# Ten adaLN sections as row sums on VectorE, in a two-layer backbone kernel on one Trainium2 core

## The chip, the core and the metric

The kernel runs on one core of a Trainium2 chip. The core has engines that work side by side, each through its own instructions in program order: TensorE (PE, matrix products), VectorE (DVE), ScalarE (ACT), GpSimd (POOL), and SyncE (SP), whose queue issues the transfers (DMA) from device memory. They meet by semaphores. The metric is the device time of one launch in microseconds. Of the kernel before there are three timed runs and one profiled execution, in which every instruction's start and length was recorded.

## What is computed

Two layers over 256 context and 256 latent tokens of width 1024. Each layer first turns two condition vectors, `c` for the latent tokens and `c_ctx` for the context, into six sections of 1024 numbers: shift, scale and gate of the mixing (0, 1, 2) and of the feed-forward part (3, 4, 5).

```python
silu_c, silu_cc = silu(c), silu(c_ctx)
for layer in range(2):
    mod_l = silu_c  @ ada_w[layer] + ada_b[layer]     # [1024] @ [1024, 6144]
    mod_c = silu_cc @ ada_w[layer] + ada_b[layer]
    sh1, sc1, g1, sh2, sc2, g2 = split(mod, 6)        # for latent and context tokens each
    h = rms_norm(x, norm1_g) * (1 + sc1) + sh1
    x = x + g1 * (concat(A(h), B(h), C(h)) @ w_out)   # three groups of attention heads
    h = rms_norm(x, norm2_g) * (1 + sc2) + sh2
    x = x + g2 * (swiglu(h) if layer == 0 else moe(h))  # dense, 2816 wide; top 2 of 8 experts
return rms_norm(x_latent, final_g)
```

`ada_w` of one layer is 1024 x 6144 floats, 24 MB; the whole of it serves two vectors.

## The kernel before

The tokens are kept feature-major (`xT`, eight k-tiles of 128 features by 512 tokens). All large products are made from high and low parts: `Weights` loads raw columns into the ring `raw` (two places), ACT copies the high part (`whi`, L219), DVE subtracts it from the raw for the low part (`wlo`, L385), and `mm3` multiplies in three passes (L645 to L647). So DVE has to make a low part of 128x512 for every k-tile of weights before PE can do the third pass of it. High and low parts have two places each.

The work is written as pieces. `add(engine, us, f, after, rank, take, give)` puts a piece on a list; `Plan`, a list scheduler with estimated durations, fixes the order: whenever an engine is free, it takes the first in rank of the pieces whose needs are met and whose buffers (`take`) are free. A smaller rank goes first. The order found is then the order of each engine's instructions and doesn't change at run time. Layer 0's mixing has ranks from 0, the pieces for its gaps 5000 (`FILL`) and on, the dense feed-forward part 6000 and on (its chunks 100 apart, each half 1000), layer 1's mixing 10000 and on. After layer 1's mixing come the experts, in an order written by hand.

The modulation is made by `ada(l, b0, nb, rings, rank, after)` for `nb` blocks of 128 columns of `ada_w[l]`. It loads eight k-tiles into tiles `idle`; PE multiplies each with `sil` (the two vectors, silu applied, as the first two of 32 columns), k-tile 4i + g into column group g of PSUM (`adap`, L442, eight matmuls in each of two pieces); ACT copies the result (`adar`); PE transposes it, one transpose a block (`adat`, L452); DVE adds the four groups (L456) and the bias (L457) into `mods[l]`. There are 42 calls:

- eight at the start, for sections 0 and 1 of layer 0, with tiles of the ring `long`;
- thirteen of two blocks each in layer 0's mixing, for its blocks 16 to 41, with rank 5000 + block and a tile of the ring `raw`;
- thirteen in the feed-forward part, twelve of three blocks and one of two, for layer 0's blocks 42 to 47 and layer 1's blocks 0 to 31: two calls follow each chunk of hidden activations and one each half of the down projection's columns, with the rank of that chunk plus 12, behind the chunk's own products and weights, and two tiles of the ring `mixC`;
- eight of two blocks in layer 1's mixing, for its blocks 32 to 47.

The dense part goes in two halves g of 1408 hidden columns; each has three chunks (gate and up products, `fsg` = silu(gate) times up at L1658, its high and low parts `fhh`, `fhl`) and then the down projection in two halves of columns, whose sums go into `xT` with the gate of `mods`.

## Time and profile before

| | |
|---|---|
| three timed runs | median 1942.58 us (1941.44 to 1943.14) |
| profiled execution, span | 1941.8 us |
| PE busy | 1904.0 us, 98% |
| DVE busy | 1427.7 us, 74% |
| ACT busy | 1170.6 us, 60% |
| DMA, mean rate | 243 GB/s |

The span runs from the first to the last recorded instruction. "Busy" is the time in which an engine executed something other than waits, branches and DMA issues; matmuls are pipelined, so that one can start before the one ahead of it ends, and the distance from start to start tells more than a single length. The page of the profile gives averages; tables by stretch of time, timelines and lists of waits are read from the trace of the same execution.

### The profile page before, as it was taken

The numbers are of one execution on the slowest core, as the hardware profiler recorded it, in microseconds if no ns is written. First come the engines' busy times: TensorE is split into PE (matmuls) and PEld (weight loads), VectorE is DVE, ScalarE is ACT, GpSimd is POOL, SyncE is SP. The second block draws the span as 40 slices with busy tenths as digits, with TensorE's granted clock in tenths as the row PEclk, the third lists the DMA queues.
The fourth block names the chain that finished last, engine by engine and source line by source line (L and its number), as shares of the span: only waits on it lengthen the run. The fifth ranks groups of instructions, "written<-read, shape, count | busy, mean of one in ns | idle before, by whom it ended". The sixth has DMA issues, their size and how long they took to land.

```text
span 1941.8 us, 27786 instructions
## 1 busy us (share of the span) xinstructions
PE 1904.0 (98%) x10317; PEld 1562.8 (80%) x10317; DVE 1427.7 (74%) x2330; ACT 1170.6 (60%) x1938; POOL 38.9 (2%) x44
## 2 busy tenths in 40 slices
PE   7999999999999999999999999999999999999998
PEld 4988678877787799887788888888888888888886
DVE  5564987433333345768889998999989999899997
ACT  4443684332222334448777777777777777777776
POOL 1001100000000000020000000000000000000000
PEclk9999999999999999999999999999999999999999
DMA  9313532435434423257799999999999999999991
GB/s 301 102 55 100 182 104 84 155 131 190 141 121 140 148 73 97 83 161 238 281 353 369 363 371 332 356 364 370 373 333 354 372 365 376 327 358 373 373 367 36
DMA packets 268911, 474.41 MB, mean 244 GB/s; under 512 B 14440, under 2 KB 75584, under 8 KB 268640
## 3 DMA queue, kind: packets, MB, share of 16 engines
q1 hardware_dynamic: 268384, 472.37, 69.6%
q8 instruction: 83, 1.36, 0.3%
q0 software_dynamic: 384, 0.19, 0.1%
q14 instruction: 60, 0.49, 0.1%
HBM read 471.47 MB, written 1.05 MB: 243 GB/s over the span
## 4 chain that ended last, share of the span: by engine, by line
PE 94%; DMA 2%; DVE 2%; ACT 1%; issue 0%; SPq 0%; DVEq 0%; ACTq 0%
PE gu L2110 32%; PE py L2135 16%; PE acc L645 9%; PE acc L647 8%; PE acc L646 8%; PE adap L442 2%; PE acc L855 2%; DMA idle<-in_ada_w 2%; PE acc L857 2%; PE acc L856 2%; PE pT L1241 1%; PE mtp L2124 1%; PE oBp L1329 1%; PE gth L2020 1%; PE sct L2159 1%; PE poC L1074 1%
## 5 line engine op out<-in xcount | busy, mean ns | idle before, releaser
L1845 DVE TENSOR_TENSOR mlo<-early,mhi 128x512 fp32r<-128x512 f32 (+1 forms) x350 | 340.0, 1019 | 24.6 <-issue 18.3
L219 ACT ACTIVATE mhi<-early 128x512 fp32r<-128x512 f32 (+1 forms) x352 | 291.3, 885 | 49.0 <-PE py L2135 25.1
L385 DVE TENSOR_TENSOR wlo<-raw,whi 128x512 fp32r<-128x512 f32 (+4 forms) x292 | 150.5, 564 | 157.8 <-ACT whi L219 157.0
L2110 PE MATMUL gu<-mlo,xh 128*128 128x512 f32 x896 | 247.9, 395 | 0.0
L219 ACT ACTIVATE whi<-raw 128x512 fp32r<-128x512 f32 (+4 forms) x292 | 134.9, 525 | 181.5 <-PE acc L646 146.5
L2110 PE MATMUL gu<-mhi,xh 128*128 128x512 f32 x896 | 244.0, 391 | 0.0
L2110 PE MATMUL gu<-mhi,xl 128*128 128x512 f32 x896 | 243.1, 390 | 0.0
L2135 PE MATMUL py<-mhi,hid 128*128 128x512 f32 x896 | 235.3, 390 | 0.0
L645 PE MATMUL acc<-hhi,whi 128*128 128x512 f32 (+1 forms) x576 | 217.6, 378 | 2.8 <-DVE rC L885 1.9
L646 PE MATMUL acc<-hlo,whi 128*128 128x512 f32 (+1 forms) x576 | 210.7, 366 | 2.2 <-DVE hlo L579 2.2
L647 PE MATMUL acc<-hhi,wlo 128*128 128x512 f32 (+1 forms) x576 | 210.6, 366 | 0.5 <-DVE wlo L385 0.5
L1845 DVE TENSOR_TENSOR mlo<-more,mhi 128x1024 fp32r<-128x1024 f32 (+1 forms) x174 | 198.5, 1184 | 11.9 <-issue 10.6
L2110 PEld LDWEIGHTS gu<-mhi,xl 128*128 128x128 f32 x896 | 168.2, 188 | 35.9
L2135 PEld LDWEIGHTS py<-mhi,hid 128*128 128x128 f32 x896 | 167.7, 188 | 35.6
L2110 PEld LDWEIGHTS gu<-mhi,xh 128*128 128x128 f32 x896 | 167.4, 188 | 34.4
L2110 PEld LDWEIGHTS gu<-mlo,xh 128*128 128x128 f32 x896 | 164.4, 188 | 31.5
L219 ACT ACTIVATE mhi<-more 128x1024 fp32r<-128x1024 f32 (+1 forms) x174 | 169.0, 1022 | 28.2 <-PE py L2135 28.2
L1845 DVE TENSOR_TENSOR mlo<-mraw,mhi 128x1024 fp32r<-128x1024 f32 (+1 forms) x116 | 132.5, 1186 | 15.6 <-ACT mhi L219 8.5
L1845 DVE TENSOR_TENSOR mlo<-spare,mhi 128x1024 fp32r<-128x1024 f32 x108 | 127.3, 1220 | 15.3 <-PE py L2135 8.0
L645 PEld LDWEIGHTS acc<-hhi,whi 128*128 128x128 f32 x576 | 108.8, 189 | 35.3 <-issue 11.2
L646 PEld LDWEIGHTS acc<-hlo,whi 128*128 128x128 f32 x576 | 108.9, 189 | 18.9 <-DVE hlo L579 3.1
L647 PEld LDWEIGHTS acc<-hhi,wlo 128*128 128x128 f32 x576 | 108.7, 189 | 18.7 <-DVE wlo L385 0.9
(371 smaller groups left out, 3035.2 us busy)
## 6 DMA issues: line engine op xcount, KB each, us to landing
early<-in_moe_w_up SPq DMA_DIRECT2D x56, 1024.0 KB, 6.0
more<-in_moe_w_up SPq DMA_DIRECT2D x54, 1024.0 KB, 6.2
early<-in_moe_w_gate SPq DMA_DIRECT2D x52, 1024.0 KB, 6.5
spare<-in_moe_w_down SPq DMA_DIRECT2D x48, 1024.0 KB, 6.0
early<-in_moe_w_down SPq DMA_DIRECT2D x112, 256.0 KB, 6.1
mraw<-in_moe_w_gate SPq DMA_DIRECT2D x27, 1024.0 KB, 6.2
mraw<-in_moe_w_down SPq DMA_DIRECT2D x27, 1024.0 KB, 5.7
more<-in_moe_w_gate SPq DMA_DIRECT2D x24, 1024.0 KB, 6.3
```

The lines of the kernel that those rows point to most:

```text
L219: act(o, i, AF.Copy)
L385: tt(l_, v, h, op=OP.subtract)
L442: mm(w["pm"][32 * g:32 * g + 32, :n], sil[:, 4 * i + g, :], w["raw"][4 * i + g], start=i == 0, stop=i == 1, tile_position=(0, 32 * g))
L645: mm(o, lh, rh, start=start, stop=False)
L646: mm(o, lh, rl, start=False, stop=False)
L647: mm(o, ll, rh, start=False, stop=stop)
L855: mm(p, t["hi"][:, kk, s], w.w[0][:, k, :], start=kk == 0, stop=False)
L856: mm(p, t["hi"][:, kk, s], w.w[1][:, k, :], start=False, stop=False)
L857: mm(p, t["lo"][:, kk, s], w.w[0][:, k, :], start=False, stop=kk == KD - 1)
L1845: tt(l, w, h, op=OP.subtract)
L2110: mm(out, a[kk // 2][:, kk % 2, o:o + 128], b[:, k, :], start=i + kk == 0, stop=i == 2 and kk == KD - 1)
L2135: mm(out, a[:, k, :], b[:, k, :], start=i + c + k == 0, stop=i == 2 and c == NCH - 1 and k == 3)
```

## The change

Sections 0 and 1 of layer 0 are made as before, by the first eight calls of `ada`. All other calls are gone: the thirteen in layer 0's mixing, the thirteen in the feed-forward part and the eight in layer 1's mixing. In their place stands `ada_rows(l, sec, rank, after)`, called in layer 0's mixing for sections 2 to 5 of layer 0 and then 0 to 5 of layer 1, ten calls, with ranks 5000 to 5009; their loads follow one another and begin behind a load of the projection's weights.

For each half of 512 columns of a section, `ada_rows` loads the eight k-tiles two at a time (512 KB, ring `adw`, two places). On DVE each k-tile is multiplied with its column of `sil`, once for each of the two vectors, and added to a running sum `adacc` (one place for a pair of sums). Then each sum is transposed in blocks of 32 x 32 and reduced over 32 columns into `adsum`. When both halves are done, one matmul with a new constant `four` (ones where row and column agree modulo 32) adds the four groups of 32 partitions, and DVE adds the bias in four instructions of 32 x 16. A section has 4 tensor_scalar, 28 scalar_tensor_tensor, 4 transposes, 4 reductions and 4 additions on DVE and one matmul on PE. An unused tile of the ring `work` is dropped, and a scratch size of the DMAs is set to 4096 bytes, which frees memory for the new rings.

```diff
@@ constants @@
+    c["four"] = p[:, None] % 32 == p[None, :] % 32
@@ kernel @@
-    plan = Plan(big=2, sm=4, hi=2, lo=2, raw=2, sp=2, work=10, long=24, mixC=2, b16=2, units=5, oC=2)
+    plan = Plan(big=2, sm=4, hi=2, lo=2, raw=2, sp=2, work=10, long=24, mixC=2, b16=2, units=5, oC=2, adw=2, adacc=1)
...
+    def ada_rows(l, sec, rank, after):
+        w = {}
+
+        def places():
+            w["r"] = small.tile([128, 2, 8, 4], F32, name="adsum", bufs=2)
+
+        last = None
+        for j in range(2):
+            c0 = sec * 1024 + j * 512
+            for k in range(0, KD, 2):
+                def load(k=k, c0=c0):
+                    w["w"] = k2.tile([128, 2, 512], F32, name="adw", tag="adw", bufs=2)
+                    w[k] = w["w"]
+                    nc.sync.dma_start(out=w[k], in_=A["ada_w"][l, k * 128:k * 128 + 256, c0:c0 + 512].rearrange("(k p) f -> p k f", p=128))
+
+                after = [add("DMA", 1.5, load, after, rank, ["adw"])]
+                for i in range(2):
+                    def summed(k=k, i=i):
+                        if k + i == 0:
+                            w["acc"] = k2.tile([128, 2, 512], F32, name="adacc", tag="adacc", bufs=1)
+                        for v in range(2):
+                            o, x, s = w["acc"][:, v], w[k][:, i], sil[:, k + i, v:v + 1]
+                            if k + i == 0:
+                                ts(o, x, s, None, op0=OP.mult)
+                            else:
+                                stt(o, x, s, o, op0=OP.mult, op1=OP.add)
+
+                    last = add("DVE", 2 * dve_us(512), summed, [*after, last, have_c], rank, ["adacc"] if k + i == 0 else (),
+                               ["adw"] if i else ())
+            for v in range(2):
+                def grouped(v=v, j=j):
...
+                    t = K2(nm="adt")
+                    nc.vector.transpose(t, w["acc"][:, v])
+                    nc.vector.tensor_reduce(w["r"][:, v, 4 * j:4 * j + 4].rearrange("p m q -> p (m q)"),
+                                            t.rearrange("p (b i) -> p b i", i=32), axis=AX.X, op=OP.add)
+
+                last = add("DVE", 2 * dve_us(512), grouped, [last], rank, ["work"], ["work"] + ["adacc"] * v)
+
+        def over_groups():
+            w["p"] = P1((128, 2, 8, 4), nm="adap")
+            mm(w["p"].rearrange("p v m q -> p (v m q)"), C("four"), w["r"].rearrange("p v m q -> p (v m q)"), start=True, stop=True)
+
+        def biased():
+            for q in range(4):
+                r = slice(32 * q, 32 * q + 32)
+                tt(mods[l][r, sec * 8:sec * 8 + 8, :], w["p"][r, :, :, q].rearrange("p v m -> p m v"),
+                   adab[l][r, sec * 8:sec * 8 + 8, None].to_broadcast([32, 8, 2]), op=OP.add)
+
+        a = add("PE", 0.25, over_groups, [last], rank, ["sm"])
+        a = add("DVE", 0.7, biased, [a, have_small], rank, (), ["sm"])
...
+        return after
@@ mixing @@
-        for b in range(EARLY if last else 16, 48 if last else 42, 2):
-            ada(l, b, 2, ["raw"], base + FILL + b, [wB[1].loaded])
+        if not last:
+            x = [wR[1].loaded]
+            for i, (m, sec) in enumerate([(0, s) for s in range(2, 6)] + [(1, s) for s in range(6)]):
+                x = ada_rows(m, sec, base + FILL + i, x)
@@ ffn @@
-        fill = [(0, b, min(3, 48 - b)) for b in range(42, 48, 3)] + [(1, b, min(3, EARLY - b)) for b in range(0, EARLY, 3)]
...
-                for x in range(2):
-                    if fill:
-                        ada(*fill.pop(0), ["mixC", "mixC"], R + 12 + x, read[-1:])
...
-                if fill:
-                    ada(*fill.pop(0), ["mixC", "mixC"], R + 12, read[-1:])
```

How this moves the instructions is shown at three places. The first is DVE in layer 0's output projection, where PE waits for the low parts `wlo` of the weights of the output projection; `adacc` are the new sums, `adw` the loaded k-tiles. Before:

```order
L385 TENSOR_TENSOR oCl_3228<-oCw_2209,oCh_3227 128x384
L385 TENSOR_TENSOR wlo_3160<-raw_2738,whi_3159 128x512
L385 TENSOR_TENSOR mBl_3065<-oBp_3232,mBh_3064 128x128
L385 TENSOR_TENSOR wlo_3160<-raw_2738,whi_3159 128x512 x2
L653 SCALAR_TENSOR_TENSOR xT_85<-oCp_3221,mods0_90,xT_85 128x256 x2
L385 TENSOR_TENSOR oCl_3282<-oCw_2209,oCh_3281 128x384
```

The same engine and place after:

```order
L711 SCALAR_TENSOR_TENSOR xT_85<-oCp_3269,mods0_90,xT_85 128x256 x2
L495 SCALAR_TENSOR_TENSOR adacc_3266<-adw_3288,sil_87,adacc_3266 128x512 x2
L386 TENSOR_TENSOR wlo_3120<-raw_1785,whi_3119 128x512
L495 SCALAR_TENSOR_TENSOR adacc_3266<-adw_3288,sil_87,adacc_3266 128x512 x2
L386 TENSOR_TENSOR wlo_3200<-raw_1867,whi_3199 128x512
L495 SCALAR_TENSOR_TENSOR adacc_3266<-adw_3299,sil_87,adacc_3266 128x512 x2
L386 TENSOR_TENSOR wlo_3120<-raw_1785,whi_3119 128x512
L495 SCALAR_TENSOR_TENSOR adacc_3266<-adw_3299,sil_87,adacc_3266 128x512 x2
```

The low parts, of which several followed one another, now have a pair of sums ahead of each.

The second place is DVE at the first chunk of the dense part, around the `fsg` of its last 128 hidden columns; `adat` is an old call's result, `raw` and `wlo` here are the chunk's gate and up weights. Before:

```order
L1658 TENSOR_TENSOR fsg_3932<-fsg_3932,acc_3962 128x512
L385 TENSOR_TENSOR wlo_4067<-raw_3947,whi_4066 128x512 x2
L385 TENSOR_TENSOR fhl_4072<-fsg_3932,fhh_4071 128x512
L385 TENSOR_TENSOR wlo_4067<-raw_3947,whi_4066 128x512 x2
L456 TENSOR_REDUCE mods0_90<-adat_4135 128x6
L457 TENSOR_TENSOR mods0_90<-mods0_90,ppar_86 128x6
L385 TENSOR_TENSOR wlo_4140<-raw_4010,whi_4139 128x512 x4
```

The same engine and place after:

```order
L1716 TENSOR_TENSOR fsg_3994<-fsg_3994,acc_4099 128x512
L495 SCALAR_TENSOR_TENSOR adacc_4197<-adw_4142,sil_87,adacc_4197 128x512 x2
L386 TENSOR_TENSOR fhl_4204<-fsg_3994,fhh_4203 128x512
L495 SCALAR_TENSOR_TENSOR adacc_4197<-adw_4177,sil_87,adacc_4197 128x512 x2
L386 TENSOR_TENSOR wlo_4185<-raw_4068,whi_4184 128x512
L495 SCALAR_TENSOR_TENSOR adacc_4197<-adw_4177,sil_87,adacc_4197 128x512 x2
L386 TENSOR_TENSOR wlo_4133<-raw_4029,whi_4132 128x512
L495 SCALAR_TENSOR_TENSOR adacc_4197<-adw_4207,sil_87,adacc_4197 128x512 x2
L386 TENSOR_TENSOR wlo_4185<-raw_4068,whi_4184 128x512
```

The old call's two small pieces are gone, and the chunk's products and low parts alternate with pairs of sums.

The third place is SP's queue of loads at the same chunk, where `idle` are the old calls' tiles. Before:

```order
L639 DMA raw_3947<-in_ffn_w_gate 128x4x512
L639 DMA raw_4010<-in_ffn_w_up 128x4x512
L431 DMA idle_4064<-in_ada_w 128x4x384
L431 DMA idle_4078<-in_ada_w 128x4x384
L639 DMA raw_4094<-in_ffn_w_up 128x4x512
```

The same queue after:

```order
L697 DMA raw_4068<-in_ffn_w_gate 128x4x512
L483 DMA adw_4093<-in_ada_w 128x2x512
L483 DMA adw_4113<-in_ada_w 128x2x512
L483 DMA adw_4142<-in_ada_w 128x2x512
...
L483 DMA adw_4231<-in_ada_w 128x2x512
L697 DMA raw_4249<-in_ffn_w_up 128x4x512
```

Between the loads of the gate and of the up weights there now stand eight loads of `adw`, each of which waits for its place in the ring.

## Rows read from the trace of the kernel before

**Rows 1.** Page: the span, and the chain that ended last by engine.

```profile
span 1941.8 us, 27786 instructions
...
PE 94%; DMA 2%; DVE 2%; ACT 1%; issue 0%; SPq 0%; DVEq 0%; ACTq 0%
```

**Rows 2.** By stage: length, busy PE, PEld, DVE, ACT, POOL; clock, DMA, GB/s.

```profile
64.00:201.00 137.00, 136.55 (x815) 118.11 (x814) 79.87 (x236) 55.92 (x149) 12.40 (x13) 1.00 0.31 91
201.00:308.00 107.00, 104.07 (x868) 76.95 (x867) 88.70 (x268) 75.97 (x230) 5.32 (x2) 1.00 0.44 135
308.00:370.00 62.00, 60.51 (x424) 55.95 (x423) 35.46 (x85) 25.68 (x54) 0.00 (x0) 1.00 0.22 74
370.00:495.00 125.00, 124.64 (x601) 93.72 (x600) 41.32 (x80) 35.49 (x67) 0.00 (x0) 1.00 0.51 171
495.00:743.00 248.00, 246.62 (x1335) 202.25 (x1334) 100.14 (x212) 76.31 (x154) 0.41 (x2) 1.00 0.37 123
860.00:930.00 70.00, 69.72 (x615) 54.79 (x614) 60.52 (x167) 52.97 (x141) 7.08 (x3) 1.00 0.75 241
```

**Rows 3.** The same for tile `adap` alone: busy PE, PEld, ACT.

```profile
201.00:308.00 107.00, 11.97 (x168) 4.02 (x168) 4.03 (x11) 1.00 0.44 135
...
860.00:930.00 70.00, 6.63 (x96) 2.42 (x96) 2.13 (x6) 1.00 0.75 241
```

**Rows 4.** Timeline of PE around an old call: start, length, instruction.

```profile
383.10 0.39 PE L647 MATMUL acc<-hhi,wlo 128*128 128x512 f32 x1
...
384.20 0.50 PE L645 MATMUL acc<-hhi,whi 128*128 128x512 f32 x1
384.54 0.39 PE L646 MATMUL acc<-hlo,whi 128*128 128x512 f32 x1
384.77 0.39 PE L647 MATMUL acc<-hhi,wlo 128*128 128x512 f32 x1
...
390.56 0.39 PE L647 MATMUL acc<-hhi,wlo 128*128 128x512 f32 x1
...
391.04 0.48 PE L645 MATMUL acc<-hhi,whi 128*128 128x512 f32 x1
```

**Rows 5.** Groups of DVE by shape: count, busy us, mean ns, idle before.

```profile
L1236 DVE TENSOR_REDUCE mx<-sB 128x2 f32<-128x1024 f32 x12 | 14.7, 1221 | 2.8 <-PE sB L1313 2.6
L1281 DVE SCALAR_TENSOR_TENSOR unit<-unit,rcA 128x512 f32<-128x512 f32 x16 | 12.1, 754 | 0.2
L1323 DVE TENSOR_SCALAR unit<-unit,smx 128x512 f32<-128x512 f32 x24 | 10.8, 482 | 0.1
L1236 DVE TENSOR_REDUCE mx<-sB 128x2 f32<-128x512 f32 x6 | 4.1, 688 | 1.2 <-PE sB L1221 1.0
```

**Rows 6.** Timeline of DVE at three places; idle time before in brackets.

```profile
244.27 0.75 DVE L1386 SCALAR_TENSOR_TENSOR qA<-qA,ang,rbA 128x512 f32<-128x512 f32 x1 [1.36 <-PE rbA L1381]
244.93 0.16 DVE L1293 RECIPROCAL r0A<-smx 128x2 f32<-128x2 f32 x1
...
275.52 0.87 DVE L1323 TENSOR_SCALAR unit<-unit,smx 128x512 f32<-128x512 f32 x2
276.31 0.15 DVE L1320 TENSOR_TENSOR esB<-mx,sink 128x2 f32<-128x2 f32 x1
...
391.32 0.18 DVE L456 TENSOR_REDUCE mods<-adat 128x6 f32<-128x24 f32 x1 [9.54 <-PE adat L452]
```

**Rows 7.** What DVE waits for, 370 to 495: total us, times, longest.

```profile
DVE wlo L385 <- ACT whi L219: 32.9, 8, 8.3
```

**Rows 8.** Loads: size of one, median us from issue to landing.

```profile
raw<-in_w_in SPq DMA_DIRECT2D x4, 512.0 KB, 3.9
raw<-in_ffn_w_down SPq DMA_DIRECT2D x4, 768.0 KB, 4.5
```

**Rows 9.** Busy time and clock (columns as rows 2), layer 1's projections.

```profile
790.00:795.00 5.00, 3.09 (x15) 2.63 (x15) 4.78 (x13) 2.95 (x6) 0.00 (x0) 0.91 0.00 0
795.00:800.00 5.00, 5.00 (x28) 4.19 (x28) 4.25 (x14) 1.94 (x7) 0.00 (x0) 0.75 0.52 153
```

More of the change, by code (lines that the diff above doesn't have):

```diff
@@ L428, in load @@
             def load(i=i, r=r):
-                t = (KT(nm="idle") if r == "long" else k2.tile([128, 1536], F32, name="idle", tag=r, bufs=2) if r == "mixC" else
-                     ring.tile([128, 2048], F32, name="idle", tag=r, bufs=2))[:, :per * n].rearrange("p (k f) -> p k f", k=per)
+                t = KT(nm="idle")[:, :per * n].rearrange("p (k f) -> p k f", k=per)
                 nc.sync.dma_start(out=t, in_=A["ada_w"][l, i * per * 128:(i + 1) * per * 128, b0 * 128:b0 * 128 + n]
@@ L466, in ada @@
         return have
+    def ada_rows(l, sec, rank, after):
[25 more added lines that the diff above has]
+                def grouped(v=v, j=j):
+                    if "r" not in w:
+                        places()
+                    t = K2(nm="adt")
[13 more added lines that the diff above has]
+        a = add("DVE", 0.7, biased, [a, have_small], rank, (), ["sm"])
+        for b in range(sec * 8, sec * 8 + 8):
+            mod[l, b] = a
+        return after
@@ L653, in gated @@
             stt(xT[:, kk, s], p[:, s], mods[l][:, 16 + kk, 1 - half:2 - half], xT[:, kk, s], op0=OP.mult, op1=OP.add)
-    wm = K2((128, 256), nm="wm")
     identb = pc.tile([128, 128], BF)
@@ L810, in trunk @@
     FILL = 5000
-    EARLY = 32
     def mixing(l, base, t, tiles, wC, started=None):
@@ L1456, in mixing @@
         read += tmajor(weights(src, [(1792, 384)], R + 150), "vC", range(4), copied, R + 150)
-        read += tmajor(weights(src, [(2176, 384)], R + 200), "rC", qts, silu_r, R + 200)
+        wR = weights(src, [(2176, 384)], R + 200)
+        read += tmajor(wR, "rC", qts, silu_r, R + 200)
         have = groupC(R + 160)
@@ L2354 @@
     from concourse.bass_utils import run_bass_kernel_spmd
-    nc = bacc.Bacc("TRN2", target_bir_lowering=False, num_devices=1)
+    nc = bacc.Bacc("TRN2", target_bir_lowering=False, num_devices=1, dynamic_dma_scratch_size=4096)
     arrays = {f"in_{n}": np.ascontiguousarray(inputs[n]) for n in _INS}
```

## The prediction

> **What bounds the kernel now.** I read the page first: PE carries 94% of the chain that ended last [rows 1]. That average speaks for any change that takes work from PE, and the change does so; but it covers stages with different limits, so the second view is the busy time of each engine by stage [rows 2]. The reader is to see two things there. PE is nearly full in every stage. VectorE (DVE) is not idle everywhere: in the first layer's attention (201 to 308 us) it works 88.7 of 107 us, in the first half of the dense FFN (370 to 495) only 41.3 of 125. The third view is what the removed work costs on PE [rows 3, 4], the fourth what the added kinds of instruction cost on DVE [rows 5, 6], the fifth who DVE waits for [rows 7].
>
> The stages are cut at marks that stand on DVE in the same order before and after: the first row maximum of attention A (201), the first residual update of the output projection (308), the first `fsg` product (370), the first residual update of the first down projection (495).
>
> **What is removed.** 34 of 42 `ada` calls. A call of two blocks is 16 PE records and two transposes; in the attention stages these fill PE's gaps: 11.97 us of PE in 201 to 308, 6.63 in 860 to 930 [rows 3]. A call of three blocks costs, in the FFN, two interruptions. The first `acc` after one starts 1.10 us after the last before it, where 0.23 us is usual, and the one behind it 0.34 instead of 0.23 later: 0.98 us each; the transposes cost 0.48 - 0.23 and, taken as behind the others, 0.11 more: 0.36 [rows 4]. So 2.3 us a call: six in 370 to 495, 13.8 us. After 495 there are two in one piece (about 1.95 each), four like the above (9.2) and one of two blocks (1.5): 14.6 us. On DVE each call removes a small reduction (0.18 us) and an addition that I take as long [rows 6]; on ACT one copy; neither is a bound.
>
> **What is added.** Ten sections, each of two halves of 512 columns. A half is 2 tensor_scalar and 14 scalar_tensor_tensor of 128x512, then 2 stream transposes and 2 reductions; a section ends with one small matmul and four 32x16 additions. DVE instructions overlap a little, so I take the step from start to start: scalar_tensor_tensor 0.66 us (244.27 to 244.93), though its mean length is 754 ns; tensor_scalar 0.395 (two in 0.79) against 482 ns [rows 5, 6]. A transpose is nowhere in this trace. Its nearest rows of 512 columns are the single-input tensor_scalar (0.48) from below and the 512-column maximum (0.69), with a 1024-column one (1.22) from above [rows 5]; I take 0.69 for it and for the reduction, which waits for it and gains no overlap. Section: 28 x 0.66 + 4 x 0.395 + 8 x 0.69 + 0.4 = 26.0 us; ten are 260 us.
>
> [...]
>
> **Where the added work lands.** Not in the idle time as a whole: DVE takes its instructions in the order in which the plan wrote them. Counting the added rows between the marks gives, with the steps above: up to 201 us 42.2 us; 201 to 308: 58 scalar_tensor_tensor, 8 tensor_scalar, 16 transposes and reductions, 53.2 us; to 370: 39.1 us; to 495: 128, 18 and 36, 117.9 us; behind it 7.1. All ten sections are thus done before the first half of the FFN ends, though layer 1 needs its own only after 740 us. The reason is in the code: their rank is 5000 and on, the FFN's is 6000 and on, so the plan lets them go ahead of the FFN's own DVE pieces, where the old calls had the FFN's rank plus 12.
>
> DVE's free time in these three stages is 18.3, 26.5 and 83.7 us, 128.5 in all [rows 2]. Even if every idle moment were filled, DVE is late by 53.2 - 3.7 (eleven calls' removed pieces) - 18.3 = 31.2; 39.1 - 26.5 = 12.6; 117.9 - 2.1 (six calls') - 83.7 = 32.1: **75.9 us**. PE can't run ahead of that: the order shows a pair of sums between any two `wlo` pieces, and the last `wlo` of the down projection stands directly ahead of the mark at 495. So in these stages the 11.97 + 13.8 us that PE is spared buy nothing; DVE's queue is what ends last.
>
> Three more terms. (a) 64 to 201 us: DVE has 57 us free and gets 42.2 (PE is full there, 136.6 of 137, and was spared almost nothing). Each sum can hold up a piece that PE needs; bounds 0 and 42, and I take 8, since the free time is larger. (b) The loads. A buffer of 512 KB lasts DVE four instructions, 2.64 us; there are two. A 512 KB load lands after 3.9 us, one of 768 KB after 4.5 [rows 8], and can start only when DVE has left the buffer. With 4.5, since the FFN's weights share the queue, DVE waits up to 1.9 us a buffer where nothing else stands between. In the attention stage the other work covers that; in 345 to 495 there are 44 buffers: 0 to 83 us. The other pieces and the transposes there come to 1.8 us a buffer, almost enough but unevenly spread; I take 20. (c) DVE's old waits, such as 32.9 us for high parts from ACT [rows 7], can't all be filled in a fixed order: 8, bounds 0 and 18.
>
> **What is still gained.** After 495 the FFN is PE's again (246.6 of 248 us, DVE 100) [rows 2]: the full 14.6 us come off. In layer 1's attention (860 to 930) DVE is busy 60.5 of 70, and the 6.63 us of PE [rows 3] and their transposes are partly filler: I take 5, bounds 0 and 9. In the expert stage nothing changes; its start shifts with the rest.
>
> **Sum.** 75.9 + 8 + 20 + 8 - 14.6 - 5 = +92.3 us on the profiled span of 1941.8: 2034. The median of the runs shown, 1942.58, lies 0.8 above the span, so 2035.
>
> **Rivals.**
> (1) The loads bound it: every buffer outside attention waits its full 1.9 us, 83 instead of 20: 2098. For it: two buffers only, and SP's queue mixes these loads with the FFN's raw weights, each waiting in order for its own ring. Against: other pieces stand between most of them. 20%.
> (2) The other side: the sums run at the single-input step. If a scalar_tensor_tensor took 0.395 and a transpose or reduction 0.40, the sums between the marks fall from 210 to 228 x 0.395 + 32 x 0.395 + 64 x 0.4 + 3 = 131 us, below the 128.5 that are free and the 5.8 that come free with the old pieces; then nothing is late, PE keeps its 14.6 + 5 and most of 25.8 in the earlier stages, and the time is about 1905. It decides from a section of 18 us down instead of 26. Against it: 0.66 is measured on a sum in place with a column as scalar, the same form as the added one [rows 6]. 5%.
> (3) The clock. [...] 10%.
> (4) The waits and the gains cancel to within 0.2% (about what a measurement of this kernel tells from no change): needs both (2) in part and no (b); 2%.
>
> **How the numbers follow.** The forecast has 63%, its own range 2005 to 2070; (1) 20%, (3) 10%, (2) 5%, (4) 2%. Low end: 75.9 and no other loss, less 14.6 and 9, less 5 if the steps are 2% shorter, gives 1990; high end: 75.9 + 20 + 60 + 12 - 14.6, gives 2096. Slower by over 0.2%: 63 + 20 + 10 = 93%; faster 5%; same 2%.
>
> **What would show it.** DVE busy above 95% from the first maximum to the first down projection, that mark at 570 to 600 instead of 495, and PE waiting there for `wlo`; `adacc` at 0.66 us a step; the stage from that mark to the second layer's norm shorter by about 15 us; idle time of DVE ahead of `adacc` that ends with a load, 20 us by the forecast and 80 by (1). It is wrong if that mark comes before 530 us, or if PE stays full up to it.

## The result and the profile after

The changed kernel takes 2047.33 us (median of four runs) against 1942.75 us for the kernel before: a ratio of 1.053 (95% interval 1.051 to 1.055). Three of the four runs took 2047 to 2048 us, among them the profiled one, and one took 2038.89. The forecast was 2035 us with a range of 1990 to 2096.

The page of the changed kernel: span, busy times, and the chain that ended last by engine.

```profile
span 2045.3 us, 27027 instructions
...
PE 1892.3 (93%) x9713; PEld 1571.7 (77%) x9713; DVE 1678.5 (82%) x2702; ACT 1160.5 (57%) x1904; POOL 38.9 (2%) x44
...
PE 77%; DVE 15%; DMA 4%; ACT 2%; issue 2%; SPq 0%; DVEq 0%; ACTq 0%
```

TensorE (PE) has lost only 12 us of busy time, VectorE (DVE) has gained 251, and the chain, 94% PE before [rows 1], now runs through DVE for 15% of a longer span. Where, the busy time by stage tells (length, busy PE, PEld, DVE, ACT, POOL, then the granted clock, DMA share, GB/s). The stages are cut at the forecast's marks, of which the last, the first update of the first half's down projection, now comes at 603.9. Behind it they are cut at the first update of that projection's second half of columns (643.7), at the first update of the second half's down projection (793.3) and at layer 1's first row maximum (964.6).

```profile
64.00:205.50 141.50, 135.70 (x782) 119.24 (x780) 126.57 (x301) 57.67 (x150) 12.40 (x13) 0.97 0.43 128
205.50:351.70 146.20, 113.71 (x691) 84.32 (x691) 134.28 (x332) 69.49 (x214) 5.32 (x2) 0.86 0.24 72
351.70:430.50 78.80, 60.41 (x401) 55.07 (x400) 74.86 (x154) 25.19 (x53) 0.00 (x0) 0.87 0.46 149
430.50:603.90 173.40, 125.44 (x506) 99.91 (x505) 158.01 (x270) 34.77 (x65) 0.00 (x0) 0.83 0.54 170
603.90:643.70 39.80, 32.92 (x134) 26.71 (x134) 18.57 (x36) 6.07 (x11) 0.00 (x0) 0.87 0.24 82
643.70:793.30 149.60, 149.60 (x662) 123.92 (x661) 51.98 (x90) 44.70 (x82) 0.00 (x0) 1.00 0.30 97
...
964.60:1054.80 90.20, 78.97 (x617) 65.10 (x616) 71.50 (x190) 65.19 (x163) 5.54 (x3) 0.98 0.49 169
```

Against [rows 2], the second to fourth rows are to be compared with 201 to 308, 308 to 370 and 370 to 495: DVE is busy 134.3 of 146.2, 74.9 of 78.8 and 158.0 of 173.4 us there, and PE has gaps and a clock of 0.83 to 0.87. From 643.7 to 793.3 PE is full again (149.6 of 149.6 us) at clock 1.00.

What the new instructions cost, the groups of DVE by shape show (count, busy us, mean ns, idle time before them):

```profile
L495 DVE SCALAR_TENSOR_TENSOR adacc<-adw,sil,adacc 128x512 f32<-128x512 f32 x280 | 195.8, 749 | 11.1 <-DMA adw<-in_ada_w 10.8
L504 DVE STREAM_TRANSPOSE adt<-adacc 128x512 f32<-128x512 f32 x40 | 28.3, 707 | 0.0
L505 DVE TENSOR_REDUCE adsum<-adt 128x16 f32<-128x512 f32 x40 | 27.4, 686 | 1.4
L493 DVE TENSOR_SCALAR adacc<-adw,sil 128x512 f32<-128x512 f32 x40 | 24.3, 652 | 4.6 <-DMA adw<-in_ada_w 4.5
```

Who waits for whom in the stage from 430.5 to 603.9 (us in all, times, longest); PE first, then DVE:

```profile
PE acc L705 <- DVE wlo L386: 29.7, 6, 12.7
PE adap L512 <- DVE adsum L505: 18.3, 1, 18.3
```

```profile
DVE adacc L495 <- DMA adw<-in_ada_w: 8.5, 5, 3.3
```

PE waits for low parts, as forecast, and once for 18.3 us at the added small matmul, for which the forecast had put down nothing. In the attention stage (205.5 to 351.7) its waits for `wlo` are smaller, 8.8 us, and those for the attention's own pieces on DVE and ACT come to some 18 us. In the stage behind (603.9 to 643.7) it waits there again:

```profile
PE adap L512 <- DVE adsum L505: 6.9, 1, 6.9
```

How the stage of layer 0's attention ends, the chain that ended last shows (start, length, what), in the changed kernel:

```profile
338.08 0.60 DVE wlo L386
...
341.97 0.61 DVE wlo L386
...
342.64 0.61 SPq L1577
...
343.30 5.69 DMA raw<-in_w_out
...
349.07 0.65 ACT wh L220
...
349.74 0.69 DVE wl L386
...
351.68 0.48 DVE xT L711
```

The last low parts of the output projection's weights come at 338 to 343; only then is a place of the ring `raw` free, the remaining weights of that projection are issued at 342.64, their transfer takes 5.69 us, and their high part, low part and product follow. In the kernel before, SyncE's queue issued these loads (tile `raw` from `w_out`) at

```profile
255.52 0.37 SPq L1512 DMA_DIRECT2D raw<-in_w_out  x1
...
277.09 18.57 SPq L1518 DMA_DIRECT2D raw<-in_w_out  x4
```

and its low parts `wlo` ran from 287 to

```profile
298.96 0.68 DVE L385 TENSOR_TENSOR wlo<-raw,whi 128x512 fp32r<-128x512 f32 x1
```

so that the transfer lay under other work: from 285 to 309 us the chain that ended last there is PE's alone.

### The profile page after: what moved, and what is told of

It reads as the page before. It is cut to its first block, busy times and chain, and to the rows that moved or that the text cites. A ratio compares the mean times of both kernels' runs of the same rounds, so it can differ in the third digit from the quotient of the medians.

```text
span 2045.3 us, 27027 instructions
## 1 busy us (share of the span) xinstructions
PE 1892.3 (93%) x9713; PEld 1571.7 (77%) x9713; DVE 1678.5 (82%) x2702; ACT 1160.5 (57%) x1904; POOL 38.9 (2%) x44
## 4 chain that ended last, share of the span: by engine, by line
PE 77%; DVE 15%; DMA 4%; ACT 2%; issue 2%; SPq 0%; DVEq 0%; ACTq 0%
PE gu L2163 30%; PE py L2188 15%; PE acc L703 6%; PE acc L705 6%; PE acc L704 6%; DVE adacc L495 5%; DVE wlo L386 2%; PE acc L911 2%; PE acc L912 1%; PE acc L913 1%; PE mtp L2177 1%; DMA idle<-in_ada_w 1%; DMA adw<-in_ada_w 1%; DVE mx L1292 1%; DVE adacc L493 1%
## 5 line engine op out<-in xcount | busy, mean ns | idle before, releaser
L220 ACT ACTIVATE whi<-raw 128x512 fp32r<-128x512 f32 (+4 forms) x292 | 134.3, 527 | 238.9 <-PE acc L704 179.9
L705 PE MATMUL acc<-hhi,wlo 128*128 128x512 f32 (+1 forms) x576 | 215.6, 374 | 37.1 <-DVE wlo L386 37.1
L495 DVE SCALAR_TENSOR_TENSOR adacc<-adw,sil,adacc 128x512 f32<-128x512 f32 x280 | 195.8, 749 | 11.1 <-DMA adw<-in_ada_w 10.8
L220 ACT ACTIVATE mhi<-more 128x1024 fp32r<-128x1024 f32 (+1 forms) x174 | 169.2, 1023 | 27.9 <-PE py L2188 27.9
L1898 DVE TENSOR_TENSOR mlo<-spare,mhi 128x1024 fp32r<-128x1024 f32 x108 | 127.4, 1222 | 15.4 <-PE py L2188 8.0
```

Of the source, the lines that this page charges most:

```text
L220: act(o, i, AF.Copy)
L495: stt(o, x, s, o, op0=OP.mult, op1=OP.add)
L705: mm(o, ll, rh, start=False, stop=stop)
L1898: tt(l, w, h, op=OP.subtract)
```

## The experiments

All stage lengths below are read between the same marks on DVE: A, layer 0's attention (forecast's 201 to 308); B, to the first `fsg` product; C, to the first update of the first down projection; D, to that of its second half of columns; E, to that of the feed-forward part's second half; F, to layer 1's first row maximum; G, to the first expert product. Behind G the experts take 990.2 to 991.0 us in every kernel whose modulation is complete; where part of it is left out, other tokens can go to other experts, and only the stages are compared.

| us | to A | A | B | C | D | E | F | G | median, whole |
|---|---|---|---|---|---|---|---|---|---|
| before | 201.0 | 107.1 | 62.0 | 125.1 | 32.0 | 163.4 | 171.9 | 89.0 | 1942.75 |
| changed | 205.5 | 146.2 | 78.8 | 173.3 | 39.8 | 149.6 | 171.3 | 90.2 | 2047.33 |
| e1 half the sums | 199.2 | 134.3 | 75.0 | 153.5 | 36.5 | 149.6 | 171.1 | 90.5 | |
| e5 no sums | 195.6 | 132.8 | 67.8 | 143.6 | 37.2 | 149.6 | 172.6 | 91.1 | |
| e2 no loads | 197.2 | 145.7 | 78.8 | 170.4 | 39.6 | 149.6 | 172.1 | 91.5 | |
| e3 small matmul later | 202.8 | 143.9 | 83.4 | 163.5 | 37.6 | 151.0 | 172.2 | 91.1 | 2038.23 |
| e4 layer 1 in rank 7400 | 199.4 | 145.4 | 74.4 | 111.8 | 29.6 | 145.7 | 175.9 | 90.4 | 1966.03 |
| e6 layer 0 later too | 205.1 | 111.1 | 79.8 | 110.5 | 27.9 | 149.4 | 178.3 | 90.7 | 1945.00 |
| e8 before, no calls in C to E | 201.2 | 106.3 | 62.2 | 110.0 | 29.9 | 149.6 | 172.0 | 89.4 | |
| e11 before, no calls in G | 201.1 | 105.8 | 63.1 | 125.1 | 32.0 | 163.4 | 172.2 | 90.9 | |
| e7 hybrid | 200.7 | 109.0 | 64.5 | 127.4 | 28.6 | 149.2 | 174.2 | 89.1 | 1935.90 |
| e9 hybrid, matmul later | 201.2 | 109.8 | 64.6 | 129.0 | 27.3 | 148.4 | 174.3 | 89.1 | 1936.20 |
| e12 hybrid, start later | 200.8 | 109.6 | 58.9 | 114.9 | 30.6 | 145.4 | 173.2 | 89.1 | 1914.88 |
| e10 hybrid, both and ranks | 200.8 | 109.9 | 58.9 | 112.2 | 28.4 | 150.2 | 172.0 | 89.1 | 1914.32 |

Seven of the kernels (e3, e4, e6, e7, e9, e10, e12) also give `adsum` of layer 1 six places of its own, where all sections shared two, and halve the DMAs' scratch to make room; the code shown below leaves that out. e3 has this with the old ranks and takes 2038.23 us. The four hybrids (e7, e9, e10, e12) also take back the old calls' tiles in the ring `raw`. Each stage length is from one profiled execution.

**Is it the amount of work on DVE?** Two kernels keep the changed kernel's order and take work out. The first halves it:

```diff
-                        for v in range(2):
+                        for v in range(1):
                             o, x, s = w["acc"][:, v], w[k][:, i], sil[:, k + i, v:v + 1]
...
+                    if v:
+                        nc.vector.tensor_copy(w["r"][:, 1, 4 * j:4 * j + 4], w["r"][:, 0, 4 * j:4 * j + 4])
+                        return
```

> The changed kernel with the sums for the context's vector left out (its sections get the latent's numbers instead): half of the scalar_tensor_tensor, tensor_scalar, transposes and large reductions; order, loads and the small matmuls stay. If VectorE's queue sets the time from 205 to 604 us, the added 210 us there fall to about 108, below the 128.5 us that were free before: the three stages (146.2, 78.8, 173.4 us in the changed kernel; 107.1, 62.0, 125.0 before) come to 300 to 315 us in all, the whole to 1935 to 1960 us. If the loads set it, or TensorE's clock, or the small matmul at which TensorE waited 52.2 us in its own order, most of the loss stays: above 2000 us.

Measured: A, B and C come to 362.8 us, not 300 to 315; before they take 294.2, changed 398.3. The three stages in this kernel (columns as above):

```profile
199.20:333.50 134.30, 107.55 (x683) 80.37 (x684) 109.41 (x295) 70.99 (x215) 5.32 (x2) 0.91 0.26 77
333.50:408.50 75.00, 60.84 (x404) 55.85 (x403) 57.73 (x128) 25.70 (x53) 0.00 (x0) 0.89 0.49 161
408.50:562.00 153.50, 124.25 (x508) 99.53 (x507) 103.67 (x188) 34.47 (x65) 0.00 (x0) 0.88 0.60 192
```

With half the sums DVE is idle for 24.9, 17.3 and 49.8 us, and two thirds of the loss (68.6 of 104.1) remained. So an overfull DVE is not the only cause. In the whole changed kernel it is still a bound of its own: there DVE works 367.2 us in three stages that took 294.2 before. Nor does the run tell how much of the rest is the order, since in C DVE now waits longer for the loads (8.5 us in the changed kernel):

```profile
DVE adacc L495 <- DMA adw<-in_ada_w: 23.4, 11, 6.3
```

The second takes out the rest of the sums:

```diff
                             if k + i == 0:
                                 ts(o, x, s, None, op0=OP.mult)
-                            else:
-                                stt(o, x, s, o, op0=OP.mult, op1=OP.add)
```

> The changed kernel with all 280 scalar_tensor_tensor of the sums left out (only the first product of each sum, the transposes, reductions and small matmuls stay; the modulation is wrong, so that other tokens go to other experts: the stages up to the experts alone are compared). The order of all the rest stays that of the changed kernel. VectorE's added work from 205 to 604 us falls from 210 us to some 59. If the amount of work were what lengthens the stage of layer 0's attention (146.2 us changed, 107.1 before, 134.3 with half the sums), it comes back to 105 to 110 us. If the order does it (low parts and loads of the output projection's weights stand behind the sums, in rank 5200 against 5000), it stays above 118 us.

Measured: A is 132.8 us, as the theory of the order had it. The busy times of A, B and C in this kernel:

```profile
195.60:328.50 132.90, 107.17 (x681) 79.75 (x680) 97.67 (x274) 71.05 (x217) 5.32 (x2) 0.91 0.22 65
328.50:396.20 67.70, 58.56 (x410) 54.13 (x409) 47.73 (x112) 26.08 (x54) 0.00 (x0) 0.95 0.53 176
396.20:539.90 143.70, 121.17 (x507) 98.29 (x506) 74.05 (x142) 34.46 (x65) 0.00 (x0) 0.90 0.62 209
```

DVE is idle for 35, 20 and 70 us, PE has gaps and a lowered clock, and the three stages still take 344.2 us, 50.0 more than before. So of the 104.1 us about half (54.1) goes with the sums, and half (50.0) stays without them, with the order, the loads and the smaller pieces as they were. How much of that is DVE's order is not shown: PE waits 9.9 us of C at the small matmul, and what the loads hold up in this kernel no run tells.

**Is it the loads?**

```diff
+    adw_once = []
...
                 def load(k=k, c0=c0):
+                    if len(adw_once) == 2:
+                        w[k] = adw_once[k // 2 % 2]
+                        return
                     w["w"] = k2.tile([128, 2, 512], F32, name="adw", tag="adw", bufs=2)
                     w[k] = w["w"]
+                    adw_once.append(w[k])
...
```

> The changed kernel with 78 of its 80 loads of adaLN weights left out (the sums read the two loaded tiles again); nothing else moves. VectorE waited 15.3 us for these loads in all, so by the forecast's theory the time falls by 5 to 15 us, to 2032 to 2042 us. If the loads bound it (through their own waits, or by holding up the weights of the feed-forward part behind them in SyncE's queue), it falls by 40 us or more, below 2005 us.

Measured, by stages, since the experts' share changes here too: A to C take 394.9 us against 398.3. Without 78 of the loads 3.4 us are gained there, and 8.3 ahead of A, most of which has another cause (the last section). With all sums in place the loads are not the bound; no run takes them out where DVE has less to do.

**Is it the small matmul in PE's queue?** The last matmul and the bias of layer 1's sections are put behind the first up product of the second half:

```diff
-        a = add("PE", 0.25, over_groups, [last], rank, ["sm"])
+        def finish(needs=()):
+            a = add("PE", 0.25, over_groups, [last, *needs], rank, ["sm"])
...
+                    if (g, ci, i) == (1, 0, 1):
+                        for f in deferred:
+                            f(read[-1:])
```

> The changed kernel with the small matmul and the bias of layer 1's six sections put behind the first up product of the feed-forward part's second half, so that TensorE doesn't stand at them; the sums stay where they were. If TensorE's waits at this matmul cost time where VectorE has ceased to be the bound, the stage between the two down projections' first updates goes from 39.8 to about 32 us and the whole to about 2039 us; if they cost in the stage to 604 us as well, by 18 us more: 2021. If they are covered, as the forecast had it (no cost for the matmul), it stays at 2047 within 3 us.

Measured: 2038.23 us, 9 less, which isn't clear of the changed kernel's own runs (one of them took 2038.89). The stages don't show the gain where the theory put it: C falls by 9.8 and D only from 39.8 to 37.6, B grows by 4.6, and 2.7 us are gained ahead of A, where nothing was moved. PE's wait of 18.3 us in C is gone, while its waits for low parts in C have grown from 29.7 us to

```profile
PE acc L713 <- DVE wlo L386: 42.4, 7, 12.5
```

Of the 18.3 us 12.7 came back as waits for low parts: most of the wait had another one behind it. For D the run is inconclusive.

**Is it the place in the order?** The same work, with other ranks. First layer 1's sections alone:

```diff
-                x = ada_rows(m, sec, base + FILL + i, x)
+                x = ada_rows(m, sec, base + FILL + i if m == 0 else 7400 + i, x)
```

> The changed kernel with one number changed: layer 1's six sections get ranks above all of the feed-forward part's (7400 and on instead of 5004 and on), so that VectorE takes their sums only where the plan has nothing else for it. The order then has 156 scalar_tensor_tensor between 205 and 604 us instead of 228, and 78 behind. If the place of the work in VectorE's queue is the cause, some 66 us leave the three stages and the later ones, where VectorE had 148 us free, don't grow: 1970 to 1985 us. If it is the work itself, wherever it stands, or its loads, it stays above 2025 us.

Measured: 1966.03 us, 81 less than the changed kernel, and lower than expected. The three stages give back 66.7 us, as expected; D, E and the stretch ahead of A give another 20, and F loses 4.6. C takes 111.8 us, less than before, and PE has no gap in it:

```profile
419.20:531.00 111.80, 111.80 (x495) 92.61 (x494) 98.93 (x163) 32.66 (x62) 0.00 (x0) 1.00 0.55 181
```

A stays at 145.4, since layer 0's sections still go ahead of the output projection there. So these next:

```diff
-                x = ada_rows(m, sec, base + FILL + i, x)
+                x = ada_rows(m, sec, 7400 + i if m else base + (FILL, 5400, 5401, 6400)[i], x)
```

> The kernel with layer 1's sections in rank 7400 and on, and now layer 0's sections 3 and 4 behind the output projection's rank (5400 and 5401 instead of 5001 and 5002), section 5 behind the first half's chunks (6400 instead of 5003). The same work on VectorE, the same loads. By the order theory the attention stage goes from 145 to 107 to 118 us, since 26 instead of 58 scalar_tensor_tensor stand in it and none ahead of the low parts; the whole goes from 1966 to 1925 to 1945 us. If the amount of work alone decides, what leaves that stage comes back in the next two (38 and 66 of these instructions there), and the whole stays at 1960 to 1970.

Measured: 1945.00 us, a ratio of 1.0005 to the kernel before (0.9995 to 1.0015). A falls to 111.1 with DVE still busy 102 us of it:

```profile
205.00:316.10 111.10, 93.75 (x682) 72.81 (x683) 102.07 (x277) 72.83 (x219) 5.33 (x2) 0.95 0.18 52
```

All ten sections and all loads are there, and DVE is busy for 1674.7 us of the whole, against 1678.5 in the changed kernel; where the sums stand was worth 102 us. That is not only a question of what stands ahead of what: DVE's work within A, B and C falls from 367.2 to 273.3 us, since sums moved to later stages, E above all. B and C:

```profile
316.10:396.00 79.90, 68.94 (x422) 61.97 (x422) 71.59 (x149) 26.19 (x54) 0.00 (x0) 0.89 0.42 136
396.00:506.50 110.50, 110.50 (x490) 91.53 (x489) 99.59 (x168) 32.32 (x61) 0.00 (x0) 1.00 0.58 183
```

PE still waits some 17 us in A for the attention's own pieces, with A only 4 us longer than before. What A gives back is lost in part in B (79.8 against 74.4), where the chain that ended last runs through sums of sections 3 and 4 before the norm, and 5.7 us are lost ahead of A, again by the effect in the last section.

**What were the old calls worth?**

```diff
-        fill = [(0, b, min(3, 48 - b)) for b in range(42, 48, 3)] + [(1, b, min(3, EARLY - b)) for b in range(0, EARLY, 3)]
+        fill = []
...
+    for m in mods:
+        nc.gpsimd.memset(m, 0.0)
...
```

> The kernel before with the feed-forward part's thirteen old calls left out and nothing in their place (their modulation stays zero, so that the experts get other tokens: the stages up to there alone are compared). By the price read off the timeline (13.8 and 14.6 us) the part of 320.5 us comes to 292 us. If a call also displaces something else (the wait for its small sums, its loads in SyncE's queue, a turn of the clock), it comes to 285 us or less.

Measured: C to E take 289.5 us instead of 320.5, so thirteen calls cost 31.0 us where the timeline's price gave 28.4. It lies between the two theories; the price from start to start missed 2.6 us.

```diff
-        for b in range(EARLY if last else 16, 48 if last else 42, 2):
+        for b in () if last else range(16, 42, 2):
...
```

> The kernel before with the eight old calls of layer 1's mixing left out and nothing in their place (sections 4 and 5 of layer 1 stay zero, so that the experts get other tokens: the stages up to there alone are compared). The forecast gave 5 us for them; in the changed kernel the stage from layer 1's first row maximum to the first expert product was 90.2 us against 89.0. If these calls only fill TensorE's gaps there, the stage stays at 88 to 91 us; if they cost and something else of the changed kernel ate the gain, it comes to 82 to 85 us.

Measured: G is 90.9 us. The eight calls in layer 1's attention cost nothing: they fill gaps of PE. That G is even 1.9 us shorter with them, no run explains.

**A version that gains.** The hybrid uses row sums only where the old calls cost something, for those of the feed-forward part; they begin in that part and have rank numbers behind its own pieces:

```diff
-        if not last:
-            x = [wR[1].loaded]
...
+        for b in range(32 if last else 16, 48 if last else 40, 2):
+            ada(l, b, 2, ["raw"], base + FILL + b, [wB[1].loaded])
...
+                    if (g, ci, i) == (0, 0, 0):
+                        x = read[-1:]
+                        for m, sec in [(0, 5)] + [(1, s) for s in range(4)]:
+                            x = ada_rows(m, sec, 7400 + sec if m else 6005, x)
```

> Row sums only for what the feed-forward part's thirteen calls made (layer 0's section 5, layer 1's sections 0 to 3), begun behind the first chunk's gate product and in ranks behind that part's own work; layer 0's sections 2 to 4 and layer 1's sections 4 and 5 by the old calls in the two attention stages. If the old calls were worth something on TensorE only in the feed-forward part and VectorE's idle time there takes the sums when they stand behind its own pieces, that part (320.5 us from the first fsg product to the second half's first update) comes to 287 to 293 us, the rest stays: 1908 to 1918 us, faster than both. If the sums cost TensorE waits wherever they stand, it is 1935 us or more.

Measured: 1935.90 us, just inside the second theory's range, 0.5% below the kernel before. But the sums don't cost waits wherever they stand: D and E are as hoped (28.6 and 149.2), and C takes 127.4 us with this wait of PE in it:

```profile
PE adap L512 <- DVE adsum L505: 17.1, 1, 17.1
```

Moving that matmul away was the next trial:

```diff
-        a = add("PE", 0.25, over_groups, [last], rank, ["sm"])
+        def finish(needs):
+            a = add("PE", 0.25, over_groups, [last, *needs], rank, ["sm"])
...
+                    if ci == 2 and i == 1:
+                        for f in deferred[g]:
+                            f(read[-1:])
```

> The hybrid (e7) with one thing changed: the small matmul of layer 0's section 5 stands some 336 matmuls later in TensorE's order (behind the first half's last up product), and layer 1's behind the same product of the second half; VectorE's order of sums stays. In e7 TensorE stood 17.1 us at this matmul in the stage from the first fsg product to the first down projection, which took 127.4 us; the clock of that stage was 0.93. If this wait is what costs there, the stage comes to 110 to 112 us and the whole to 1917 to 1921 us. If the sums hold up the low parts anyway, the wait only moves to the next low part: the stage stays above 122, the whole above 1930.

Measured: 1936.20 us, C 129.0. The wait moved to the next low part, as the second theory had it:

```profile
PE acc L710 <- DVE wlo L386: 15.3, 2, 13.0
```

Next, several things at once, against e9: a later start, and larger rank numbers, which come later, for section 5 and for the small matmuls.

```diff
+        late = 7205 if l else 6205
...
-                    if (g, ci, i) == (0, 0, 0):
+                    if (g, ci, i) == (0, 0, 1):
...
-                            x = ada_rows(m, sec, 7400 + sec if m else 6005, x)
+                            x = ada_rows(m, sec, 7400 + sec if m else 6205, x)
```

> As e9, with the sums begun one product later (behind the first chunk's up product, so that none stands ahead of the first fsg product), section 5's sums in rank 6205 instead of 6005, and the small matmuls in rank 6205 and 7205. In e7 the stage of the output projection's second half and the norm took 64.5 us against 62.0 before, with 14 sums in it, and the stage behind the feed-forward part 174.2 against 171.9, with three of the small matmuls in it. If those sums and matmuls are the cause, both go back by about 2 us each: 3 to 5 us below e9, 1912 to 1917 us. If not, it is as e9 within 2 us.

Measured: 1914.32 us, a ratio of 0.985 (0.983 to 0.987). The number lies in the expected range by luck: the reckoning was 3 to 5 us below e9, and it came 21.9 below. C falls by 16.8 us, of which nothing had been expected, B by 5.7 and F by 2.3, where about 2 each had been. PE is full and at full clock in C, D and E:

```profile
369.60:481.80 112.20, 112.20 (x498) 92.92 (x497) 94.51 (x159) 32.32 (x61) 0.00 (x0) 1.00 0.56 181
481.80:510.10 28.30, 28.30 (x127) 23.44 (x126) 25.13 (x44) 6.07 (x11) 0.00 (x0) 1.00 0.62 204
510.10:660.40 150.30, 150.30 (x668) 124.59 (x667) 110.11 (x199) 44.55 (x82) 0.00 (x0) 1.00 0.47 151
```

The last run takes the later start alone, against e7:

```diff
-                    if (g, ci, i) == (0, 0, 0):
+                    if (g, ci, i) == (0, 0, 1):
```

> The hybrid (e7) with only the start of the sums moved: behind the first chunk's up product instead of its gate product; ranks and small matmuls as in e7. In e9 the wait of 17.1 us at the small matmul became waits of 15.3 us for low parts, because VectorE was busy with sums without a gap from 370 to 395 us, where the first fsg products, their low parts and the next chunk's low parts are due. If sums in that stretch are the cause, the first half's stage falls from 127.4 to 112 to 114 us with this alone, and the whole to 1914 to 1921 us. If e10 owed it to the lower ranks (section 5's sums, the small matmuls), it stays at 124 us or more, the whole above 1930 us.

Measured: 1914.88 us, 0.985 (0.983 to 0.987). The start is the cause: it alone brings 21.0 us, and e10 is only 0.6 below. C falls by 12.5 us (somewhat less than expected), B by 5.6 and E by 3.8, while D grows by 2.0. The 26 us from 369 to 395, the end of B and the beginning of C, first in e7, then in e12:

```profile
369.00:395.00 26.00, 8.87 (x40) 7.01 (x38) 25.28 (x41) 4.62 (x9) 0.00 (x0) 0.75 0.41 126
```

```profile
369.00:395.00 26.00, 26.00 (x117) 21.53 (x115) 19.20 (x31) 7.91 (x14) 0.00 (x0) 1.00 0.51 174
```

In e7 DVE is busy 25.28 of 26 us and PE 8.87; in e12 DVE still works 19.20 us and PE 26.00. Over the whole of C, DVE had 13 us to spare in e7; what PE needed in these 26 us stood behind sums of which the first were due at the first down projection, 100 us later.

## Why the prediction was right, and where it was not

**The size and the sign** were right, and so was the place: the span grew by 103.5 us (forecast 92.3), of which 4.5 come before A, 104.1 in A to C, 7.8 in D, -13.8 in E, -0.6 in F, 1.2 in G and 0.2 in the experts. The mark at the first down projection came at 603.9 us (570 to 600 forecast), and PE waited for `wlo`, though in A more for the attention's own pieces. DVE was busy for 92% of A to C, where above 95% had been named as the sign.

**The prices of the instructions** held: a pair of sums takes 1.32 us from start to start, 0.66 each; a transpose 707 ns and its reduction 686, where 690 had been taken for both. The four small additions take 0.71 us, where 0.4 had been taken. The sums in the chain at the end of A:

```profile
330.98 1.32 DVE adacc L495 x2
```

DVE's busy times by the forecast's addition come to 138.2, 74.6 and 157.1 us for the three stages; the trace has 134.3, 74.9 and 158.0.

**The 8 us ahead of A**, for sums that hold up other pieces, look right against the measured 4.5, but that is luck. The profile of e4, whose DVE and GpSimd have the same instructions in the same order up to A, reaches A at 199.4 us, before the 201.0 of the kernel before: there the sums cost nothing. What cost 6.1 us in the changed kernel's profile is the collision in the last section.

**The step that failed is the price in "even if every idle moment were filled, DVE is late by 75.9".** It takes the loss for the part of the added work that exceeds the idle time. As a lower bound the formula holds: DVE works 367.2 us in three stages that took 294.2 before, so that with all sums there 73.0 us could not be avoided by any order. As a price it fails, because it lets the idle time hide the rest. By that formula half the sums would cost 53.2/2 - 3.7 - 18.3 = 4.6 us in A and nothing in B and C; measured were 68.6 in the three. Without the scalar_tensor_tensor it gives nothing; measured were 50.0. Idle time on an engine that takes its instructions in order is no budget: the same sums cost no more than the old calls in one order (e6, level with the kernel before) and 104 us more in another, by where they stand. The forecast had the reason in hand (rank 5000 against the feed-forward part's 6000), and did not draw from it that the output projection's weights (rank 5200) stand behind the sums as well. So the two causes overlap, and the forecast knew one of them. That 103.9 (75.9 + 20 + 8) met the measured 104.1 in A to C is in part luck.

**The loads** were put at 20 us between 0 and 83. DVE waited 8.5 us for them in C and not at all in A and B, and leaving them out gained 3.4 us there. Rival (1) is out. DVE's idle time of all kinds in A to C is 11.9 + 3.9 + 15.4 = 31.2 us, against 20 + 8 in the sum.

**The gain behind the first down projection** was put at 14.6 us. E did fall by 13.8. D grew by 7.8 instead: sums were left over there (the forecast counted their 7.1 us and gave them no price), and PE stood 6.9 us at the small matmul in its own queue. "One small matmul" costs some 0.3 us where it runs (its two records, 217 to 476 ns each, took 0.33 us together at 190.08) and up to 18.3 us where it waits, with all of PE's work queued behind it; that term was missing. Whether D would come back fully without it, e3 did not settle.

**The gain in layer 1's attention** (5 us) was wrong. The forecast took the old calls there to be partly on the path; G is 90.2 us without them in the changed kernel, and 90.9 with them left out of the kernel before. PE's 98% of busy time hid that these calls ran in time that PE had to spare.

**The clock**, to which the forecast gave 10% as rival (3), is there: 0.86, 0.87, 0.83 and 0.87 in A to D, where PE was busy for 113.7 of 146.2, 60.4 of 78.8, 125.4 of 173.4 and 32.9 of 39.8 us, and 1.00 in E, where it was full. In C 506 matmuls took 125.44 us, 0.248 each; in e4 495 took 111.80, 0.226 each. That is 11 us of PE's time in C. How much of it moved the end, where PE was waiting for DVE anyway, no run separates; that stays open. In every stage printed above of the changed kernel and of the experiments with a clock below 1.00, PE has gaps; in [rows 9] the clock is lower in the 5 us behind a gap than in the 5 us with it. By what rule it is granted, no run here shows.

**Rival (2)**, sums at the single-input step, is out by the 0.66 us.

## What to carry to other kernels

An engine's idle time doesn't tell what new work costs that stands ahead of what the bound engine waits for: before counting free microseconds, look in the order at what comes behind each new instruction, give it a place behind everything that feeds the bound engine, and begin it after the change of stage, where that engine's next inputs are made. Moving one start by one product was worth 21 us here, and changing ranks 102 us, with the same work. Price the removed work by stage too: thirteen such calls cost 31 us where PE was the bound, eight cost nothing where they filled its gaps, and the best version, 1.5% faster than the kernel before, moved only the former.

## What the hardware showed that was not expected

Two tensor_scalar on DVE and a memset on GpSimd did not run side by side. The changed kernel's timeline, GpSimd and then DVE (start, length, instruction):

```profile
190.07 6.96 POOL L1246 MEMSET qmA<- 128x4096 f32 x2 [40.50 <-PE acc L704]
```

```profile
189.62 7.70 DVE L493 TENSOR_SCALAR adacc<-adw,sil 128x512 f32<-128x512 f32 x2
197.24 0.71 DVE L517 TENSOR_TENSOR mods<-adap,ppar 32x16 f32<-32x16 f32 x4
```

Two tensor_scalar that elsewhere take 0.88 us together (in e7 at 376.72) took 7.70 and ended at 197.32, 0.29 us behind the memset (190.07 + 6.96 = 197.03). In the kernel before the same memset ran from 192.66 to 199.63, and DVE's tensor_tensor beside it kept their length (0.42 us; all six `rt<-qB` there take 417 ns on average):

```profile
192.66 6.97 POOL L1190 MEMSET qmA<- 128x4096 f32 x2 [37.85 <-PE acc L646]
```

```profile
195.27 0.42 DVE L1165 TENSOR_TENSOR rt<-qB,cst 128x256 f32<-128x256 f32 x1
195.60 0.42 DVE L1165 TENSOR_TENSOR rt<-kB,cst 128x256 f32<-128x256 f32 x1
```

Some 6.8 us of DVE's time (7.70 - 0.88) went that way, just ahead of A. Why the two did not run side by side, no run here shows. It did not happen in every kernel: in e4, with the same instructions in the same order on both engines up to A, the memset began 0.2 us later, and DVE was not held up, with 0.87 us for the pair:

```profile
190.26 7.22 POOL L1246 MEMSET qmA<- 128x4096 f32 x2 [40.51 <-PE acc L704]
```

```profile
189.68 0.87 DVE L493 TENSOR_SCALAR adacc<-adw,sil 128x512 f32<-128x512 f32 x2
```

e4 reaches A 6.1 us earlier than the changed kernel. In e6 the two tensor_scalar took 7.62 us, in e3 4.21 and in e2 0.87, and these kernels reach A at 205.1, 202.8 and 197.2 us. So differences of some microseconds ahead of A say nothing about the loads or the ranks that the experiments change.
